# A two-layer diffusion step on one core: w_ffn_in token by token, with the activations stationary and the weights moving, and TensorE transposes behind it

## The chip, the cores and the metric

The kernel runs on 1 core of one Trainium2 chip. The metric is the device time of one execution in microseconds; less is better. The time of the kernel before is the median of 3 runs.

## The reference, cut to what matters

Two layers run over 128 context tokens and 128 latent tokens, 256 tokens in all, with D_MODEL = 2048 and D_FF = 5632. The change lies in the feed-forward part at the end of each layer:

```python
h = rms_norm(x, lp['ln_ffn']) * (1.0 + sc2) + sh2
gate, up = jnp.split(h @ lp['w_ffn_in'], 2, axis=-1)
x = x + g2 * ((jax.nn.silu(gate) * up) @ lp['w_ffn_out'])
```

All data are float32. `w_ffn_in` is 2048 x 11264 and `w_ffn_out` 5632 x 2048 in each layer.

## The kernel before

**Layout.** Activations lie transposed in SBUF: channels on the 128 partitions, the 256 tokens along the row (`xT`, 16 tiles of 128 channels). A matrix product gives out the transposed result, 128 output channels on the partitions and 256 tokens along the row, so that the next product can contract over channels again.

**Three products for one.** Every large product is split into a high and a low part. ScalarE rounds a weight tile `w` to `wh` (`act`, L155), VectorE takes `wl = w - wh` (`tt`, L128), in `weights`. The activations come as `hh` and `hl` (for `w_ffn_in`) or `ah` and `al` (for `w_ffn_out`). `block` in `gemm_steps` then issues three matmuls for one output: high by high, low activations by high weights, high activations by low weights. Each matmul instruction is two on TensorE, a load of the stationary operand (PEld) and the stream of the moving one (PE).

**`gemm_steps`.** It takes the rows of the weight matrix in tiles of 128 (16 steps for `w_ffn_in`), each up to 1024 columns wide. A step fetches and converts the tile of the next step, issues the matmuls of its own and may run a piece of another stream (`mod_tick`). Sums stay in up to four PSUM banks `pg` (pool `ps_g`, 4 buffers) through all steps. In the last step (`tail`) the banks are finished one after the other and each is handed to the evict function. A plan's entry (bank, offset, width, kind, column) says what a block does: kind `"w"` holds 128 weight columns stationary and moves 256 tokens; kind `"t0"` or `"t1"` holds 128 tokens stationary and moves `width` weight columns. `w_in` has used the second kind all along for the two banks of the GLA values (32 steps in the two layers), with 512 columns.

**The feed-forward part** (L1161 to L1217) goes through D_FF in three segments of 16, 16 and 12 tiles of 128 channels, and a segment in two groups of n = 8, 8 or 6 tiles. Each group is one product for the gate columns and one for the up columns, 128 n columns each. `ev_gate_ff` puts Silu of a gate bank into `sg` (ScalarE). `ev_up` multiplies `sg` by the up bank (VectorE), rounds it to `ah` (ScalarE) and takes `al` (VectorE). After both groups two products with `w_ffn_out` use `ah` and `al` as they are.

**Order of the work.** Each engine runs its own list in order; a framework sets the lists from the program's order and its own estimates. Weight tiles arrive through five buffers and are converted into five pairs `wh`, `wl`. Beside the products, VectorE works through the modulation matrices (`macc`, L288), four instructions for each slice of 128 rows, at a rate that `mod_tick` counts in weight tiles.

Of the kernel before, what the change touches and what calls it, by code (L numbers as in the profile page):

```python
# [17 lines left out]
KT = D // 128  # L18
# [85 lines left out]
def tile_backbone(ctx, tc, T, O):  # L104
# [22 lines left out]
    def tt(out, a, b, op):  # L127
        r = nc.vector.tensor_tensor(out=out, in0=a, in1=b, op=op)  # L128
        dve["last"] = r.ins.name
        return r  # L130
# [16 lines left out]
    def act(out, a, func=AF.Copy, **k):  # L147

        name = table_of.get(func)
        if name is not None and name != table["name"]:  # L150
            ld = nc.scalar.preload_act_table_set(name)
            for u in table["users"]:
                tc.add_manual_dep(ld.ins, u, no_sync, reason="table")
            table.update(name=name, load=ld.ins.name, users=[])
        r = nc.scalar.activation(out=out, in_=a, func=func, **k)  # L155
        if name is not None:
            tc.add_manual_dep(r.ins, table["load"], no_sync, reason="table")
            table["users"].append(r.ins.name)
        return r
# [8 lines left out]
    def px(shape):  # L168
        return ps_x.tile(shape, F32, tag="x", name="px")
# [85 lines left out]
    def early_run(l, m, kts, after):  # L255

        ps, w = early[l, m]
        for kt in kts:
            wv = quads(w[kt])
            for q in range(4):  # L260
                r = mm(ps[32 * q:32 * q + 32, :], sc[:, kt], wv[:, q], start=(kt == 0), stop=False)
                tc.add_manual_dep(r.ins, after, no_sync, reason="order")
# [84 lines left out]
    def gemm_steps(cols, tiles, x, plan, evict, pieces=None, pre=None, tail=1, quiet=0, done=None):  # L347

        ncol = sum(ap.shape[1] for ap in cols)
        nb = max(p[0] for p in plan) + 1  # L350
        banks = [ps_g.tile([128, 512], F32, tag="g", name="pg") for _ in range(nb)]
        byb = [[p for p in plan if p[0] == b] for b in range(nb)]
        nt = len(tiles)
        ahead = []

        def fetch(ti):
            if ti < nt:
                ahead.append(weights(cols, tiles[ti][0], ncol, pieces))

        def block(b, ti, wh, wl, a, c):  # L360
            ps = byb[b]
            for i, (_, off, width, kind, lc) in enumerate(ps):
                o = banks[b][:, off:off + width]
                if kind == "w":
                    sh, sl = wh[:, lc:lc + 128], wl[:, lc:lc + 128]
                    trip = ((sh, a), (sh, c), (sl, a))
                else:
                    t = slice(int(kind[1]) * 128, int(kind[1]) * 128 + 128)
                    mh, ml = wh[:, lc:lc + width], wl[:, lc:lc + width]
                    trip = ((a[:, t], mh), (c[:, t], mh), (a[:, t], ml))  # L370
                for j, (lt, rh) in enumerate(trip):
                    mm(o, lt, rh, start=(ti == 0 and i == 0 and j == 0),
                       stop=(ti == nt - 1 and i == len(ps) - 1 and j == 2))

        fetch(0)
        held = []
        for ti, (row, kt) in enumerate(tiles):
            fetch(ti + 1)
            wh, wl = ahead.pop(0)
            if pre is not None:  # L380
                pre(kt)
            a, c = x(kt)
            if ti >= nt - tail:
                held.append((ti, wh, wl, a, c))
            else:
                for b in range(nb):
                    block(b, ti, wh, wl, a, c)
            if ti < nt - quiet:
                mod_tick(ncol / 1024)
            yield  # L390
        for b in range(nb):
            for h in held:
                block(b, *h)
            if done is not None and b == nb - 1:
                done()
            evict(b, banks[b])
        dve["evict"] = dve["last"]

    def gemm(*args, **kw):
        for _ in gemm_steps(*args, **kw):  # L400
            pass
# [18 lines left out]
    def k_tiles(order):  # L420
        return [(128 * i, i) for i in order]

    def plan_w(n, lc0=0, b0=0):
        return [(b0 + i // 2, (i % 2) * 256, 256, "w", lc0 + 128 * i) for i in range(n)]
# [44 lines left out]
    def norm_mod(pool, l, msc, msh):  # L469
        new_h()  # L470
        hh, hl = normed["hh"], normed["hl"]

        def pre(k):
            t = pool.tile([128, 256], F32, tag="nt", name="nt", bufs=2)
            for g in range(2):
                s = slice(g * 128, g * 128 + 128)
                b = modv[:, l, msh, k, g:g + 1]
                stt(t[:, s], xT[:, k, s], modv[:, l, msc, k, g:g + 1], rstd[:, s], ALU.mult, ALU.mult)
                act(hh[:, k, s], t[:, s], AF.Identity, bias=b)
                stt(hl[:, k, s], t[:, s], b, hh[:, k, s].bitcast(F32), ALU.add, ALU.subtract)  # L480
        return pre
# [509 lines left out]
    for l in range(DEPTH):  # L991
# [168 lines left out]

        with PR(f"ff{l}") as fp:  # L1161
            f0 = 0
            for seg, nkt in enumerate((16, 16, 12)):
                parts = []
                done_kt = 0
                while done_kt < nkt:
                    n = 8 if nkt == 16 else 6
                    c0 = f0 + 128 * done_kt
                    sg = {}

                    def ev_gate_ff(b, bank):
                        sg[b] = fp.tile([128, 512], F32, tag="sg", name="sg", bufs=5)
                        act(sg[b], bank, AF.Silu)

                    def ev_up(b, bank):
                        ah = fp.tile([128, 2, 256], F32R, tag="ah", name="ah", bufs=8)
                        al = fp.tile([128, 2, 256], F32R, tag="al", name="al", bufs=8)
                        parts.append((ah, al))
                        s = sg[b]
                        tt(s, s, bank, ALU.mult)  # L1180
                        sv = s.rearrange("p (a t) -> p a t", a=2)
                        act(ah, sv)
                        tt(al, sv, ah.bitcast(F32), ALU.subtract)

                    pre = norm_mod(fp, l, 4, 3) if f0 == 0 and done_kt == 0 else None
                    w = T["w_ffn_in"][l]
                    gemm([w[:, c0:c0 + 128 * n]], k_tiles(range(KT)), hT, plan_w(n), ev_gate_ff, pre=pre, quiet=16 if pre else 0)
                    gemm([w[:, D_FF + c0:D_FF + c0 + 128 * n]], k_tiles(range(KT)), hT, plan_w(n), ev_up)
                    done_kt += n

                def aT(k):
                    h, lo = parts[k // 2]
                    return h[:, k % 2], lo[:, k % 2]

                if seg == 0:
                    mod_flush((l, 5))
                last_seg = seg == 2
                if last_seg:
                    ss = SquareSum(fp, l == DEPTH - 1)
                    if l == DEPTH - 1:  # L1200
                        yt = accp.tile([128, 2, D], F32, tag="macc", name="yt")
                for r in range(2):
                    def ev_ff(b, bank, r=r):
                        k = 8 * r + 2 * b
                        residual(l, 5, bank, k)
                        if last_seg:
                            ss.add(k, on_pe=(k >= KT - 6), last=(k == KT - 2))
                            if l == DEPTH - 1:
                                final_transpose(fp, k, yt)

                    tiles = [(f0 + 128 * i, i) for i in range(nkt)]
                    nxt = last_seg and r and l < DEPTH - 1
                    if nxt:
                        early_load(l + 1, 3)
                    gemm([T["w_ffn_out"][l][:, 1024 * r:1024 * r + 1024]], tiles, aT, plan_w(8), ev_ff, tail=2 if last_seg and r else 1,
                         quiet=QUIET if nxt else 0,
                         done=(lambda: early_run(l + 1, 3, range(1), pe["last"])) if nxt else None)  # L1217
                f0 += 128 * nkt
            mod_flush(*ffd)
            if l < DEPTH - 1:  # L1220
                early_run(l + 1, 3, range(1, EARLY), pe["last"])
                rsq(rstd, ss.ps, ss.acc[:, 0:256])
            else:
                final_scale(fp, ss, yt)
# [31 lines left out]
```

## Time and profile before

| | |
|---|---|
| median of 3 runs | 2512.47 us (2510.18 to 2515.29) |
| the profiled execution's own time | 2501.59 us |
| its span in the trace | 2499.6 us |
| TensorE matmul (PE) busy | 2442.9 us, 98% of the span |
| TensorE weight load (PEld) busy | 2245.2 us, 90% |
| VectorE (DVE) busy | 1656.6 us, 66% |
| ScalarE (ACT) busy | 1031.2 us, 41% |
| granted TensorE clock, mean | 0.997 |

The busy time of PE is the time in which at least one matmul was under way. Matmuls overlap: one lasts far longer than the distance to the next, so what a matmul costs in a stream is the distance between two starts. The profiled execution was 10.9 us shorter than the median of the runs.

### The profile page before, as it was taken

What the parts mean: (1) busy time and instruction counts of PE and PEld (TensorE: products, weight loads), DVE (VectorE), ACT (ScalarE), POOL (GpSimd) and SP (SyncE); (2) the same over time, 40 slices, a digit from 0 to 9 for tenths busy, and PEclk for the clock granted to TensorE, in tenths of its full rate; (3) what the DMA queues carried; (4) which work ended last, traced back from release to release, by engine and by line L of the source; (5) the groups of instructions that cost most, each with busy time, mean ns of one, the idle gap of its engine ahead of it and who ended that gap; (6) DMA issues with size and microseconds to landing.
All of it is one profiled execution on the core that took longest, in us unless ns stands there. A gap on an engine that the chain in (4) does not pass through costs nothing.

```text
span 2499.6 us, 47125 instructions
## 1 busy us (share of the span) xinstructions
PE 2442.9 (98%) x19685; PEld 2245.2 (90%) x19685; DVE 1656.6 (66%) x2367; ACT 1031.2 (41%) x1405; POOL 0.2 (0%) x4
## 2 busy tenths in 40 slices
PE   6999999999999999999999999999999999999998
PEld 3666767999999999999998887899999999999998
DVE  3665555887879888888858555598655545454455
ACT  2334433454443334334446444345444334433443
POOL 0000000000000000000000000000000000000000
PEclk9999999999999999999999999999999999999999
DMA  8988788867778778677956667686755566555662
GB/s 302 334 311 307 279 296 319 330 222 250 244 244 295 263 250 303 226 266 264 318 197 195 220 221 257 236 308 202 236 178 184 179 186 186 178 187 167 183 202 96
DMA packets 167304, 601.20 MB, mean 241 GB/s; under 512 B 18576, under 2 KB 24882, under 8 KB 146612
## 3 DMA queue, kind: packets, MB, share of 16 engines
q1 hardware_dynamic: 164104, 592.27, 70.3%
q10 hardware_dynamic: 2988, 5.93, 0.7%
q8 instruction: 154, 2.52, 0.4%
q14 instruction: 58, 0.48, 0.1%
HBM read 592.03 MB, written 6.09 MB: 239 GB/s over the span
## 4 chain that ended last, share of the span: by engine, by line
PE 93%; DMA 4%; DVE 2%; ACT 1%; issue 0%; SPq 0%; ACTq 0%; DVEq 0%
PE pg L164 81%; PE px L164 8%; PE mps L164 4%; DMA mw<-in_w_mod_dram 3%; DMA xin<-in_x_prompt_dram 0%; DVE wl L128 0%; PE px L948 0%; ACT e L155 0%; DVE xT L133 0%; DMA rows<-in_ln_ffn_dram 0%; ACT wh L155 0%; DMA w<-in_w_in_dram 0%; PE px L977 0%; DVE st L934 0%; DMA rows<-in_hy_filt_b_dram 0%
## 5 line engine op out<-in xcount | busy, mean ns | idle before, releaser
L128 DVE TENSOR_TENSOR wl<-w,wh 128x1024 fp32r<-128x1024 f32 (+3 forms) x816 | 872.1, 1085 | 579.4 <-ACT wh L155 573.6
L155 ACT ACTIVATE wh<-w 128x1024 fp32r<-128x1024 f32 (+3 forms) x816 | 767.0, 949 | 1130.7 <-PE pg L164 975.3
L164 PE MATMUL pg<-hh,wh 128*128 128x256 f32 x3648 | 1039.0, 286 | 3.7 <-ACT hh L155 2.6
L164 PE MATMUL pg<-hl,wh 128*128 128x256 f32 x3648 | 1034.7, 284 | 0.0
L164 PE MATMUL pg<-hh,wl 128*128 128x256 f32 x3648 | 1032.2, 284 | 2.5 <-DVE wl L128 2.5
L164 PEld LDWEIGHTS pg<-hh,wh 128*128 128x128 f32 x3648 | 696.6, 191 | 41.6 <-issue 26.1
L164 PEld LDWEIGHTS pg<-hl,wh 128*128 128x128 f32 x3648 | 697.9, 191 | 10.4 <-issue 8.8
L164 PEld LDWEIGHTS pg<-hh,wl 128*128 128x128 f32 x3648 | 696.5, 191 | 11.5 <-issue 6.8
L164 PE MATMUL pg<-ah,wl 128*128 128x256 f32 x1408 | 395.3, 281 | 0.0
L164 PE MATMUL pg<-al,wh 128*128 128x256 f32 x1408 | 395.3, 281 | 0.0
L164 PE MATMUL pg<-ah,wh 128*128 128x256 f32 x1408 | 395.1, 282 | 0.0
L288 DVE SCALAR_TENSOR_TENSOR macc<-mw,sc,macc 128x1024 f32<-128x1024 f32 x268 | 331.6, 1278 | 0.5 <-DMA mw<-in_w_mod_dram 0.5
L164 PEld LDWEIGHTS pg<-ah,wh 128*128 128x128 f32 x1408 | 264.7, 188 | 1.7 <-ACT wh L155 1.7
L164 PEld LDWEIGHTS pg<-al,wh 128*128 128x128 f32 x1408 | 265.6, 189 | 0.1
L164 PEld LDWEIGHTS pg<-ah,wl 128*128 128x128 f32 x1408 | 264.8, 188 | 0.1
L164 PE MATMUL mps<-mw,sc 128*32 128x512 f32 (+1 forms) x1216 | 143.1, 537 | 17.7 <-DMA mw<-in_w_mod_dram 17.7
L164 PEld LDWEIGHTS mps<-mw,sc 128*32 128x32 f32 x1216 | 29.7, 112 | 73.6 <-issue 36.8
L133 DVE SCALAR_TENSOR_TENSOR xT<-pg,modv,xT 128x128 f32<-128x128 f32 x256 | 69.6, 342 | 27.4 <-PE pg L164 27.3
L164 PE MATMUL pg<-ymh,wh 128*128 128x256 f32 x256 | 72.3, 286 | 1.9 <-DVE xT L133 1.9
L164 PE MATMUL pg<-ymh,wl 128*128 128x256 f32 x256 | 71.5, 283 | 0.6 <-DVE wl L128 0.6
L164 PE MATMUL pg<-yml,wh 128*128 128x256 f32 x256 | 72.1, 283 | 0.0
L164 PEld LDWEIGHTS pg<-ymh,wh 128*128 128x128 f32 x256 | 48.8, 192 | 5.1 <-issue 2.9
(285 smaller groups left out, 1838.1 us busy)
## 6 DMA issues: line engine op xcount, KB each, us to landing
mw<-in_w_mod_dram SPq DMA_DIRECT2D x160, 1024.0 KB
w<-in_w_ffn_in_dram SPq DMA_DIRECT2D x256, 512.0 KB
w<-in_w_ffn_out_dram SPq DMA_DIRECT2D x176, 512.0 KB
w<-in_w_ffn_in_dram SPq DMA_DIRECT2D x128, 384.0 KB
mw<-in_w_mod_dram SPq DMA_DIRECT2D x64, 512.0 KB
w<-in_w_in_dram SPq DMA_DIRECT2D x64, 512.0 KB
w<-in_w_out_dram SPq DMA_DIRECT2D x64, 512.0 KB
w<-in_w_in_dram SPq DMA_DIRECT2D x64, 256.0 KB
```

The lines of the kernel that those rows point to most:

```text
L128: r = nc.vector.tensor_tensor(out=out, in0=a, in1=b, op=op)
L133: r = nc.vector.scalar_tensor_tensor(out=out, in0=a, scalar=s, in1=b, op0=op0, op1=op1)
L155: r = nc.scalar.activation(out=out, in_=a, func=func, **k)
L164: r = nc.tensor.matmul(*args, **kw)
L288: r = nc.vector.scalar_tensor_tensor(out=acc[:, i, cs], in0=w[:, cs], scalar=c, in1=acc[:, i, cs], op0=ALU.mult, op1=ALU.add)
```

## The change

`w_ffn_in` uses the second kind of block: the 128 tokens of each half (t0: context, t1: latent) are held stationary, and up to 512 weight columns move. A bank now holds 128 tokens on the partitions and 512 (n = 8) or 384 (n = 6) channels along the row; there are four banks for either n (before: three for n = 6). `w_ffn_out` needs channels on the partitions again, so `turn` transposes each finished 128 x 128 piece on TensorE into a PSUM tile `px` and makes `ah` and `al` from there. The four turns of a group are kept in a list `late`; `run_late` runs one after each step of the following products, from the second step on.

```diff
             f0 = 0
+            late = []
+
+            def run_late(steps):
+
+                for i, _ in enumerate(steps):
+                    if late and i:
+                        late.pop(0)()
+
...
+                    wd = 64 * n
+
                     def ev_gate_ff(b, bank):
                         sg[b] = fp.tile([128, 512], F32, tag="sg", name="sg", bufs=5)
-                        act(sg[b], bank, AF.Silu)
+                        act(sg[b][:, :wd], bank[:, :wd], AF.Silu)
 
                     def ev_up(b, bank):
-                        ah = fp.tile([128, 2, 256], F32R, tag="ah", name="ah", bufs=8)
-                        al = fp.tile([128, 2, 256], F32R, tag="al", name="al", bufs=8)
-                        parts.append((ah, al))
                         s = sg[b]
-                        tt(s, s, bank, ALU.mult)
-                        sv = s.rearrange("p (a t) -> p a t", a=2)
-                        act(ah, sv)
-                        tt(al, sv, ah.bitcast(F32), ALU.subtract)
-
+                        tt(s[:, :wd], s[:, :wd], bank[:, :wd], ALU.mult)
+                        late.append(lambda: turn(b, s))
+
+                    def turn(b, s, n=n, wd=wd, halves=[None, None]):
+
+                        t, half = divmod(b, 2)
+                        if t == 0:
+                            ah = fp.tile([128, 4, 256], F32R, tag="ah", name="ah", bufs=4)
+                            al = fp.tile([128, 4, 256], F32R, tag="al", name="al", bufs=4)
+                            halves[half] = ah, al
+                            parts.extend((ah[:, j], al[:, j]) for j in range(n // 2))
+                        ah, al = (v[:, :n // 2, 128 * t:128 * t + 128] for v in halves[half])
+                        p = px([128, 4, 128])[:, :n // 2]
+                        for j in range(n // 2):
+                            nc.tensor.transpose(p[:, j], s[:, 128 * j:128 * j + 128], ident)
+                        act(ah, p)
+                        tt(al, p, ah.bitcast(F32), ALU.subtract)
+
+                    plan = [(2 * t + i, 0, wd, f"t{t}", wd * i) for t in range(2) for i in range(2)]
...
-                    gemm([w[:, c0:c0 + 128 * n]], k_tiles(range(KT)), hT, plan_w(n), ev_gate_ff, pre=pre, quiet=16 if pre else 0)
-                    gemm([w[:, D_FF + c0:D_FF + c0 + 128 * n]], k_tiles(range(KT)), hT, plan_w(n), ev_up)
+                    run_late(gemm_steps([w[:, c0:c0 + 128 * n]], k_tiles(range(KT)), hT, plan, ev_gate_ff, pre=pre, quiet=16 if pre else 0))
+                    run_late(gemm_steps([w[:, D_FF + c0:D_FF + c0 + 128 * n]], k_tiles(range(KT)), hT, plan, ev_up))
...
                 def aT(k):
-                    h, lo = parts[k // 2]
-                    return h[:, k % 2], lo[:, k % 2]
+                    return parts[k]
```

The products with `w_ffn_out` keep their plan and are driven by `run_late` too.

On TensorE's list, in a step of `w_ffn_in` with n = 8, these rows stand before the change (moving operand first behind the arrow, then the stationary one; the numbers tell buffers apart). A bank takes six of them and a step has four banks:

```order
L164 MATMUL pg_5398<-hh_5394,wh_5926 128x256
L164 MATMUL pg_5398<-hl_5395,wh_5926 128x256
L164 MATMUL pg_5398<-hh_5394,wl_5927 128x256
L164 MATMUL pg_5399<-hh_5394,wh_5926 128x256
L164 MATMUL pg_5399<-hl_5395,wh_5926 128x256
L164 MATMUL pg_5399<-hh_5394,wl_5927 128x256
```

With the change, the end of the second step of the second group's gate product, the first turn of the first group's `sg` and the start of the third step read:

```order
L164 MATMUL pg_6132<-wh_6141,hh_5394 128x512
L164 MATMUL pg_6132<-wh_6141,hl_5395 128x512
L164 MATMUL pg_6132<-wl_6142,hh_5394 128x512
L1202 MATMUL px_6177<-ident_81,sg_5791 128x128 x4
L164 MATMUL pg_6129<-wh_6159,hh_5394 128x512
L164 MATMUL pg_6129<-wh_6159,hl_5395 128x512
L164 MATMUL pg_6129<-wl_6160,hh_5394 128x512
```

Three rows of 512 columns stand where six of 256 stood, weights and activations have changed sides, and four transposes stand between two steps.

On VectorE's list these rows stood at the end of the first group's up product in layer 0:

```order
L128 TENSOR_TENSOR sg<-sg,pg 128x512
L128 TENSOR_TENSOR wl<-w,wh 128x1024
L128 TENSOR_TENSOR al<-sg,ah 128x512
L128 TENSOR_TENSOR sg<-sg,pg 128x512 x3
L128 TENSOR_TENSOR al<-sg,ah 128x512 x3
L128 TENSOR_TENSOR wl<-w,wh 128x1024
L288 SCALAR_TENSOR_TENSOR macc<-mw,sc,macc 128x1024 x4
L128 TENSOR_TENSOR wl<-w,wh 128x1024 x8
```

With the change the same place reads:

```order
L128 TENSOR_TENSOR sg<-sg,pg 128x512
L128 TENSOR_TENSOR wl<-w,wh 128x1024
L128 TENSOR_TENSOR sg<-sg,pg 128x512 x3
L128 TENSOR_TENSOR wl<-w,wh 128x1024
L288 SCALAR_TENSOR_TENSOR macc<-mw,sc,macc 128x1024 x4
L128 TENSOR_TENSOR al<-px,ah 128x4x128
L128 TENSOR_TENSOR wl<-w,wh 128x1024 x2
L128 TENSOR_TENSOR al<-px,ah 128x4x128
```

The four multiplications stay where they were, and the four subtractions for `al` have moved behind the block of `macc` and between the conversions of later weight tiles.

## Rows read from the trace of the kernel before

**Rows 1.** The page, busy time (us), share of the span and instructions of an engine.
```profile
PE 2442.9 (98%) x19685; PEld 2245.2 (90%) x19685; DVE 1656.6 (66%) x2367; ACT 1031.2 (41%) x1405; POOL 0.2 (0%) x4
```
**Rows 2.** The chain that ended last, in order of time: start us, us, what.
```profile
542.95 115.61 PE pg L164 x960
...
660.42 194.00 PE pg L164 x1632
...
1837.01 609.17 PE pg L164 x5082
```
**Rows 3.** Timeline of PE, w_ffn_in, layer 0: start us, us, engine, line, instruction.
```profile
1236.01 0.28 PE L164 MATMUL pg<-hh,wh 128*128 128x256 f32 x1
...
1236.97 0.28 PE L164 MATMUL pg<-hh,wl 128*128 128x256 f32 x1
```
**Rows 4.** Timeline of PE, w_in, layer 1: GLA values between weight-stationary blocks.
```profile
1364.61 0.40 PE L164 MATMUL pg<-wh,hh 128*128 128x512 f32 x1
...
1366.00 0.28 PE L164 MATMUL pg<-hh,wh 128*128 128x256 f32 x1
...
1402.24 0.40 PE L164 MATMUL pg<-wh,hh 128*128 128x512 f32 x1
1402.48 0.39 PE L164 MATMUL pg<-wh,hl 128*128 128x512 f32 x1
...
1403.61 0.28 PE L164 MATMUL pg<-hh,wh 128*128 128x256 f32 x1
```
**Rows 5.** Timeline of PE, attention of layer 1: a run of 384-column matmuls.
```profile
1395.15 0.34 PE L164 MATMUL px<-kyl,uk 128*128 128x384 f32 x1
...
1397.07 0.40 PE L164 MATMUL px<-uk,kyh 128*128 128x256 f32 x2
```
**Rows 6.** Timeline of PE, attention of layer 1: transposes between matmuls.
```profile
1406.43 0.82 PE L948 MATMUL px<-ident,e 128*128 128x128 f32 x6
1407.01 0.36 PE L164 MATMUL pg<-hh,wh 128*128 128x256 f32 x1
1407.21 0.28 PE L164 MATMUL pg<-hl,wh 128*128 128x256 f32 x1
...
1381.84 0.76 PE L948 MATMUL px<-ident,e 128*128 128x128 f32 x5
1382.35 0.47 PE L164 MATMUL pg<-wh,hh 128*128 128x512 f32 x1
1382.66 0.39 PE L164 MATMUL pg<-wh,hl 128*128 128x512 f32 x1
```
**Rows 7.** Instructions of line 977: duration of one in ns, min/median/max, first and last start.
```profile
L977 PE MATMUL px<-ident,xl x32: 270/273/328, 2446.0 to 2489.9; 128*128 128x128 f32 x32
```
**Rows 8.** Timeline of DVE at the end of the first up product, layer 0.
```profile
633.40 0.69 DVE L128 TENSOR_TENSOR sg<-sg,pg 128x512 f32<-128x512 f32 x1 [1.40 <-PE pg L164]
...
635.74 1.88 DVE L128 TENSOR_TENSOR sg<-sg,pg 128x512 f32<-128x512 f32 x3
...
640.47 4.87 DVE L288 SCALAR_TENSOR_TENSOR macc<-mw,sc,macc 128x1024 f32<-128x1024 f32 x4
645.26 4.62 DVE L128 TENSOR_TENSOR wl<-w,wh 128x1024 fp32r<-128x1024 f32 x4
```
**Rows 9.** Windows: from:to, us, busy and count of PE, PEld, DVE, ACT, POOL; PEclk, DMA share, GB/s.
```profile
870.00:990.00 120.00, 120.00 (x1003) 120.00 (x1002) 104.59 (x94) 49.07 (x50) 0.00 (x0) 1.00 0.81 284
1110.00:1230.00 120.00, 120.00 (x1001) 119.94 (x1000) 107.25 (x108) 53.64 (x66) 0.00 (x0) 1.00 0.83 293
...
760.00:810.00 50.00, 50.00 (x429) 50.00 (x428) 46.74 (x53) 19.12 (x18) 0.00 (x0) 1.00 0.82 291
```
**Rows 10.** Groups by line and shape, 487 to 1313 us: busy, mean ns | idle before, releaser.
```profile
L155 ACT ACTIVATE sg<-pg 128x512 f32<-128x512 f32 x22 | 13.0, 590 | 0.8
L128 DVE TENSOR_TENSOR sg<-sg,pg 128x512 f32<-128x512 f32 x22 | 14.2, 683 | 7.5 <-PE pg L164 7.5
```

More of the change, by code (lines that the diff above doesn't have):

```diff
@@ L1214, in tile_backbone @@
                         early_load(l + 1, 3)
-                    gemm([T["w_ffn_out"][l][:, 1024 * r:1024 * r + 1024]], tiles, aT, plan_w(8), ev_ff, tail=2 if last_seg and r else 1,
+                    run_late(gemm_steps([T["w_ffn_out"][l][:, 1024 * r:1024 * r + 1024]], tiles, aT, plan_w(8), ev_ff, tail=2 if last_seg and r else 1,
                          quiet=QUIET if nxt else 0,
-                         done=(lambda: early_run(l + 1, 3, range(1), pe["last"])) if nxt else None)
+                         done=(lambda: early_run(l + 1, 3, range(1), pe["last"])) if nxt else None))
                 f0 += 128 * nkt
```

## The prediction

> **What bounds the kernel now.** I read the busy times first: TensorE has a matmul under way for 2442.9 of 2499.6 us, VectorE is busy for 66% and ScalarE for 41% [rows 1]. So only what TensorE does can shorten the run, as long as the others keep up. The chain of waits in order of time says the same of the feed-forward part: the pieces there are TensorE alone, 194.0 us and 609.2 us without a break, across w_ffn_in and w_ffn_out alike [rows 2]. Nothing is waited for there, so the change is worth what it takes from or adds to TensorE's own stream.
>
> In that stream a matmul lasts 280 ns, but the next one starts long before it ends; the cost is the distance between starts. In w_ffn_in eight distances make 0.96 us, 120.0 ns for 256 columns [rows 3]. A window inside one such product counts 1003 in 120 us, of which two or three only reach in over the edges [rows 9]. The piece of 960 that holds the start of the layer gives 115.61 / 960 = 120.4 ns [rows 2]. I use 120.0.
>
> **What goes and what comes on TensorE.** w_ffn_in has 88 column tiles of 128, 16 row tiles, 3 products, 2 layers: 8448 matmuls of 256 columns, 1013.8 us. Of these 6144 belong to groups with n = 8 and 2304 to n = 6. The change makes 3072 matmuls of 512 columns from the first and 1536 of 384 columns from the second. The columns moved are as many as before, the instructions fewer by 3840.
>
> *512 columns.* The trace has this very form, in w_in: weights moving, hh and hl stationary, six in a row between blocks of the old form. One run takes 1366.00 - 1364.61 = 1.39 us for six, 231.7 ns each; another 1403.61 - 1402.24 = 1.37 us, 228.3 ns, and the last five of it, behind the step over from the old form, 1403.61 - 1402.48 = 1.13 us, 226 ns [rows 4]. In the changed kernel the form goes on for 44 us at a time, and runs of six always hold the step over. So I take the faster run, 228.3 ns, and keep 226 and 231.7 as bounds. Saved: 6144 x 0.1200 - 3072 x 0.2283 = 737.3 - 701.3 = **36.0 us** (25.5 to 43.0).
>
> *384 columns.* A run of them in the attention goes from 1395.15 to 1397.07 in 11 distances (the rows between count ten more), 174.5 ns [rows 5]. Saved: 2304 x 0.1200 - 1536 x 0.1745 = 276.5 - 268.0 = **8.4 us**. Its bounds are small beside the others.
>
> *Transposes.* 44 channel tiles, two token halves, two layers: 176 of 128 x 128, in 32 turns of four and 16 of three. I price them with the step over to them and back. Six of them start at 1406.43 and the second matmul behind them at 1407.21; that is 0.78 us less the one distance of 0.12 that would be there anyway, 0.66 us or 110 ns each. Five ahead of a 512-column matmul: 1382.66 - 1381.84 = 0.82 less 0.23, 0.59 us or 118 ns each [rows 6]. I take 115 ns: 176 x 0.115 = **20.2 us** added (19.4 to 20.8).
>
> Here a rule of the Trainium skill speaks against the change. The rows give 110 to 118 ns for a transpose in a stream [rows 6], although one lasts 273 ns from start to end [rows 7]. The Trainium skill (TensorE: Matmul & The Clock Gate, Part 4: PE-mode transpose) gives about 275 ns for a transpose in a kernel's context. By 275 ns they would cost 48.4 us, an estimate from that page, and the change would lose some 4 us. The trace agrees with 275 as the time from start to end and not as the distance.
>
> **What moves on the other engines, priced at nothing.** The rounding to ah, the subtraction for al, Silu and the multiplication are as many elements as before; ah and al now read PSUM.
>
> - *VectorE keeps up.* In w_ffn_in of layer 0 it is busy for 104.59 of 120 us with n = 8 and 107.25 of 120 with n = 6 [rows 9]. The same work in a time shorter by 4.9% and 3.1% makes 92% of both. In w_ffn_out it is at 46.74 of 50 us, 93%, and TensorE is at work for all 50 of them [rows 9]. So the trace already shows a stage as tight as the new one without a wait. The DMA share, 0.81 and 0.83, rises to 0.86 at most.
> - *The turn finds its data.* At the end of an up product VectorE starts its first multiplication as bank 0 ends, and the last three are done by 635.74 + 1.88 = 637.62, 4.2 us later [rows 8]; with al moved behind, about 3.6 us. TensorE meanwhile finishes three banks (9 x 0.228 = 2.1 us) and two steps of the next product (2 x 2.74 us) before its first transpose, 7.5 us behind bank 0. The cover is 3.9 us. Behind the turn, the next matmul needs wl; VectorE's block of four macc (4.87 us, then conversions from 645.26, 11.9 us behind bank 0 [rows 8]) stands where it stood, and fewer instructions are ahead of it now.
> - *Four banks for n = 6.* There is no spare bank any more. A bank must be read before the next product starts on it, 9 x 0.1745 = 1.57 us later. ScalarE needs 0.59 us and VectorE 0.68 us for it [rows 10]. If a macc instruction (4.87 / 4 = 1.22 us) has just begun, it is 1.9 us, 0.3 us late: 4 up products, 1.3 us at most. I take 0.
>
> **Sum.** 36.0 + 8.4 - 20.2 = 24.2 us less, with bounds 25.5 + 8.4 - 20.8 - 1.3 = 11.8 and 43.0 + 8.4 - 19.4 = 32.0. The profiled execution of 2501.6 us becomes 2477.4 us. That execution was 10.9 us shorter than the median of the runs, 2512.5 us, so the forecast for a median is **2488 us**, with 2480 to 2501 by the bounds. A measurement of this kernel can tell some 0.2%, 5 us, from no change.
>
> **Rivals.**
>
> 1. *Each transpose costs its whole length.* If the matmul behind a transpose had to wait for its end, 176 x 0.273 = 48.0 us [rows 7] would meet a gain of 44.4 us: 3.6 us slower, 2516 us, within 0.2%. (It is what the rule of the Trainium skill, TensorE: Matmul & The Clock Gate, Part 4, comes to.) Against it stand both runs of rows 6; for it, that none of them has four transposes ahead of a long stream. 5%.
> 2. *The pace is set by columns, not by instructions.* Should the long stream of 512 take twice 120 ns, and 384 columns 180, nothing is saved, and the transposes remain: 20.2 us slower, 2533 us. It decides from 512 columns at 240 - (20.2 - 8.4) / 3.072 = 236.2 ns on, with 384 as priced. For it: the old form itself does not keep one pace; in w_ffn_out the same 256 columns go at 50 / 427, 117 ns [rows 9], so something beside the form matters, and stationary activations may bring their own. Against it: the runs of six lie at 228 to 232 with hh and hl stationary [rows 4]. 9%.
> 3. *VectorE comes late to the turns.* If it reaches the multiplications later by more than the cover of 3.9 us, TensorE stands at the first turn of each of the 12 groups. One block of macc too late (4.87 us [rows 8]) costs 1.0 us a group, 12 us: 2500 us, still faster. To undo the gain it takes 2 us in each group. Against it: VectorE itself waited 7.5 us for TensorE ahead of its multiplications in layer 0 [rows 10], so it comes early. 8% that it takes enough to land within 0.2%, or a little behind.
>
> **How the numbers follow.** The forecast's own case has 78%: it holds 2480 to 2501. Rival 1 has 5%, rival 2 9%, rival 3 8%. The range for 8 in 10 is 2476 to 2505: the bounds, and 4 us on either side for the scatter of medians (the runs before span 5.1 us). Faster by over 0.2% (under 2507): the 78% and a part of rival 3, 81%. Within 0.2%: rival 1 and most of rival 3, 9%. Slower: rival 2 and the end of rival 3, 10%.
>
> **What the changed profile would show.** Right: in w_ffn_in starts of 512-column matmuls 226 to 232 ns apart and of 384 ones near 174, granted clock 1.0; a turn of four transposes puts 0.45 us between two steps; the chain in the feed-forward part is still TensorE alone, the part of layer 0 shorter by some 12 us, that of layer 1 by as much. Wrong: a pace over 236 ns; idle time of PE ahead of px with VectorE's sg as releaser, or ahead of pg with wl; starts behind a transpose 0.27 us apart; a granted clock under 1.0 in these stretches.

## The result and the profile after

The changed kernel takes 2475.87 us (median of 4 runs, 2474.91 to 2477.44). The kernel before took 2513.88 us beside it (4 runs, 2510.18 to 2518.00). The ratio is 0.9848, with a 95% interval of 0.9834 to 0.9863: **faster, by 38 us in this comparison**. The forecast was 2488 us with a range from 2476 to 2505; the time lies 12.1 us below the forecast and 0.13 us below the lower end of the range. The profiled execution took 2476.38 us.

The page of the kernel after gives the busy times that answer to [rows 1]:

```profile
PE 2416.0 (98%) x16021; PEld 2094.0 (85%) x16021; DVE 1657.0 (67%) x2375; ACT 1026.8 (41%) x1413; POOL 0.2 (0%) x4
```

3664 instructions are gone from TensorE: 3840 matmuls fewer, 176 transposes more. It is still at work for 98% of the span, so the time came out of its own stream, and none of it went into idle time. TensorE's waits from 487 to 1300 us, the feed-forward part of layer 0 and a little ahead of it (waiting engine and line, for whom: us in total, times, longest), are these three and no more:

```profile
PE pg L164 <- DVE xT L133: 1.9, 2, 1.7
PE pg L164 <- DVE wl L128: 0.6, 1, 0.6
PE pg L164 <- DVE nt L133: 0.6, 1, 0.6
```

None is for `sg` ahead of a turn, and the single wait for `wl` is 0.6 us. In layer 1, from 1600 us to the end, there are three waits more, the longest of 1.0 us, and none of them is for `sg`, `wl` or a turn. The chain that ended last (start us, us, what) answers to [rows 2]:

```profile
549.18 92.88 PE pg L164 x408
642.07 0.44 PE px L1202 x4
642.50 2.76 PE pg L164 x12
645.26 0.44 PE px L1202 x4
...
733.34 0.44 PE px L1202 x4
733.78 2.85 PE pg L164 x24
```

It is TensorE alone, as before, now cut by the turns (a *turn* is the group of three or four transposes that `turn` issues). The first 408 matmuls of 512 columns take 92.88 / 408 = 227.6 ns each, the start included. A turn of four takes 0.44 us; the turns of a segment's last group stand in `w_ffn_out`, where a step has 24 matmuls of 256 columns.

The timeline of PE (start us, us, engine, line, instruction) shows a turn, then a stretch of 512 columns and one of 384 far from any turn:

```profile
641.67 0.40 PE L164 MATMUL pg<-wl,hh 128*128 128x512 f32 x1
641.90 0.60 PE L1202 MATMUL px<-ident,sg 128*128 128x128 f32 x4
642.26 0.48 PE L164 MATMUL pg<-wh,hh 128*128 128x512 f32 x1
642.57 0.39 PE L164 MATMUL pg<-wh,hl 128*128 128x512 f32 x1
...
899.81 0.39 PE L164 MATMUL pg<-wh,hh 128*128 128x512 f32 x1
...
904.57 0.39 PE L164 MATMUL pg<-wh,hh 128*128 128x512 f32 x1
...
1139.73 0.33 PE L164 MATMUL pg<-wl,hh 128*128 128x384 f32 x1
...
1143.89 0.33 PE L164 MATMUL pg<-wl,hh 128*128 128x384 f32 x1
```

Between 899.81 and 904.57 lie 21 distances: **226.7 ns** each, where the forecast took 228.3 (in longer stretches, of 300 to 480 matmuls and behind the first five of each, it is 226.7 to 227.0, and I use 226.9). Between 1139.73 and 1143.89 lie 24: **173.3 ns**, against 174.5. The windows answer to [rows 9] (columns as there):

```profile
870.00:990.00 120.00, 120.00 (x539) 99.16 (x538) 105.92 (x94) 50.16 (x52) 0.00 (x0) 1.00 0.83 292
1110.00:1230.00 120.00, 120.00 (x708) 119.86 (x707) 107.77 (x111) 55.45 (x71) 0.00 (x0) 1.00 0.84 294
```

The granted clock is 1.00 in both, as before. VectorE is at 88% and 90%, the DMA share at 0.83 and 0.84, TensorE without a gap.

A stretch goes from the start of a product's first matmul to the start of the next product's (the last one to the end of the span). Summed over its six stretches, `w_ffn_in` went from 1020.5 to 980.2 us and `w_ffn_out` from 532.9 to 543.3 us: 30 us in all, 14.3 in layer 0 and 15.7 in layer 1, where the forecast had some 12 in each. `w_ffn_out` became longer because half of the turns stand in it, 9.7 us by their rows.

### The profile page after: what moved, and what is told of

Same layout as the page of the kernel before. It is cut to its first block, busy times and chain, and to the rows that moved or that the text cites. A ratio compares the mean times of both kernels' runs of the same rounds, so it can differ in the third digit from the quotient of the medians.

```text
span 2474.4 us, 39841 instructions
## 1 busy us (share of the span) xinstructions
PE 2416.0 (98%) x16021; PEld 2094.0 (85%) x16021; DVE 1657.0 (67%) x2375; ACT 1026.8 (41%) x1413; POOL 0.2 (0%) x4
## 4 chain that ended last, share of the span: by engine, by line
PE 93%; DMA 4%; DVE 2%; ACT 1%; issue 0%; SPq 0%; DVEq 0%; ACTq 0%
PE pg L164 79%; PE px L164 8%; PE mps L164 4%; DMA mw<-in_w_mod_dram 3%; PE px L1202 1%; DVE wl L128 0%; PE px L948 0%; ACT e L155 0%; DMA w<-in_w_in_dram 0%; DVE xT L133 0%; DMA fdec<-in_decay_dram 0%; DVE nt L133 0%; ACT wh L155 0%; PE px L977 0%; DVE st L934 0%
## 5 line engine op out<-in xcount | busy, mean ns | idle before, releaser
L128 DVE TENSOR_TENSOR wl<-w,wh 128x1024 fp32r<-128x1024 f32 (+3 forms) x816 | 873.4, 1086 | 549.1 <-ACT wh L155 543.3
L164 PE MATMUL pg<-wh,hh 128*128 128x512 f32 (+1 forms) x1600 | 597.2, 374 | 1.1 <-DVE nt L133 1.1
L164 PE MATMUL pg<-wh,hl 128*128 128x512 f32 (+1 forms) x1600 | 595.6, 372 | 0.0
L164 PE MATMUL pg<-wl,hh 128*128 128x512 f32 (+1 forms) x1600 | 594.5, 372 | 0.0
L164 PEld LDWEIGHTS pg<-wh,hl 128*128 128x128 f32 x1600 | 300.5, 188 | 41.0 <-issue 0.3
L164 PE MATMUL pg<-hh,wh 128*128 128x256 f32 x832 | 244.3, 295 | 2.6 <-ACT hh L155 1.3
L164 PE MATMUL pg<-hh,wl 128*128 128x256 f32 x832 | 236.8, 288 | 3.7 <-DVE wl L128 3.7
L164 PE MATMUL pg<-hl,wh 128*128 128x256 f32 x832 | 239.0, 288 | 0.0
L164 PEld LDWEIGHTS pg<-hh,wh 128*128 128x128 f32 x832 | 159.2, 192 | 35.4 <-issue 26.7
L164 PEld LDWEIGHTS pg<-hh,wl 128*128 128x128 f32 x832 | 158.5, 192 | 13.3 <-issue 6.8
L164 PEld LDWEIGHTS pg<-hl,wh 128*128 128x128 f32 x832 | 159.7, 192 | 10.8 <-issue 9.4
```

The costliest lines, as they stand in the source:

```text
L164: r = nc.tensor.matmul(*args, **kw)
```

## The experiments

**The theory**: the gain is TensorE's stream alone, fewer matmuls at a fixed cost beside their columns, less some 110 ns for each transpose; what goes beyond it comes from the draw of the runs, that is from which executions a median happens to hold. **The rivals**: a transpose costs more than its place in the stream; it is the form (activations stationary), not the number of matmuls, that pays; the kernel before was slower in some stage at the timed runs than in its profile; the changed kernel has a longer head of its own. *Head* is the time from the start to the first product of `w_ffn_in` in layer 0, in which the change alters no instruction of TensorE; the rest is the span less the head.

### Both kernels again, unchanged

Seven runs, without an edit. The first two:

> The kernel before, unchanged, profiled and timed once more. In the two profiles the changed stages gave back 30 us, the spans 25 us and the timed medians 38 us; this run asks where the other differences lie. Theory H (the head varies): the part ahead of the first product of w_ffn_in, 543.0 us in the profile of before and 549.2 in that of after though nothing in it is changed, differs from execution to execution, and the first profile of before caught a short one. Then this profile's span is longer than 2499.6 by just what its head is longer, with 1956.6 us from the head's end to the end, and the timed runs spread over 8 us or more. Rival P (timed runs of the kernel before are longer than profiled ones): the profile is near 2500 again with a head near 543, and the timed median near 2513. Rival S (the stages themselves vary): the part behind the head is longer than 1956.6 by more than 3 us.

> The changed kernel, unchanged, once more. Theory H: behind the head 1925.2 us as in its first profile, a head that may differ from 549.2 by some us, the span by the same. Rival P: span 2474 and median 2476 with the same head. Rival S: the part behind the head differs by more than 3 us.

After a third time, beside more runs of before:

> The changed kernel, unchanged, a third time, beside more runs of the kernel before. In its two profiles the head waited 20.0 and 18.4 us for the modulation weights, in the two of before 14.0 and 14.0. Theory H (chance): a head like before's turns up, near 543 us, and the difference of the medians is 28 to 33 us. Rival P (the changed program has a head that is longer by 4 us whenever it runs): head near 549 again.

And each kernel twice more, in turn on one chip:

> The kernel before once more, unchanged, for its head: the time from the start to the first product of w_ffn_in, in which both kernels issue the same instructions. So far it ended at 543.0 and 545.9 us in two profiles of before and at 549.2, 550.2 and 548.0 in three of after. Theory C (chance): the head varies from execution to execution whatever the kernel, and four looks in turn on one chip overlap: this one ends its head anywhere from 543 to 551 us. Rival K (the kernel): the changed kernel has a longer head of its own; then this one ends at 543 to 546 and both looks at after at 548 to 551. In both, what lies behind the head takes 1957 us, within 1.5.

> The changed kernel once more, unchanged. Theory C: the head ends anywhere from 543 to 551 us. Rival K: 548 to 551. In both, what lies behind it takes 1925 to 1928 us.

> The kernel before a second time on the same chip. Theory C: head anywhere from 543 to 551 us, and the two heads of before differ from one another by as much as from those of after. Rival K: 543 to 546, 3 us or more ahead of both looks at after. Behind the head 1957 us, within 1.5.

> The changed kernel a second time on the same chip. Theory C: head anywhere from 543 to 551 us. Rival K: 548 to 551. Behind the head 1925 to 1928 us. If K holds, the change gives 28 us and not 31; if C holds, 31 us is what it gives, and the rest of the measured difference is the draw of the runs.

Measured by time: 2508.69 us for before again (11 runs, ratio to before 1.0004, 0.9995 to 1.0013), 2480.07 us for after again (4 runs beside 18 of before at 2508.66; ratio 0.9883, 0.9870 to 0.9896) and 2475.85 us for after once more (5 runs beside 11 of before at 2509.12; ratio 0.9877, 0.9861 to 0.9893). So three comparisons give 38.0, 28.6 and 33.3 us. By profile, us:

| profiled execution | time | span | head | rest |
|---|---|---|---|---|
| before | 2501.59 | 2499.6 | 542.95 | 1956.6 |
| r1_before_again | 2505.65 | 2503.6 | 545.89 | 1957.7 |
| s1_before | 2516.46 | 2514.4 | 552.51 | 1961.9 |
| s3_before | 2510.04 | 2508.0 | 548.45 | 1959.6 |
| after | 2476.38 | 2474.4 | 549.18 | 1925.2 |
| r2_after_again | 2480.03 | 2478.1 | 550.21 | 1927.9 |
| r3_after_once_more | 2474.93 | 2473.0 | 547.98 | 1925.0 |
| s2_after | 2483.12 | 2481.2 | 553.60 | 1927.6 |
| s4_after | 2476.22 | 2474.4 | 545.93 | 1928.5 |

The end of the head is the start of one row of the chain; for the longest head of before and the shortest of after:

```profile
552.51 115.61 PE pg L164 x960
```

```profile
545.93 92.88 PE pg L164 x408
```

The heads of the two kernels overlap (543.0 to 552.5, and 545.9 to 553.6), so a head that is always longer with the change is out; a difference of 1 or 2 us in the mean isn't excluded by nine heads. Expectations were missed on the way: r3_after_once_more was to show a head near 543 us if chance alone were at work, and showed 548.0, so that only the four runs in turn decided; and two heads of these lie beyond the 551 us expected. The head is the largest part of what varies from one execution of a kernel to the next. The rest was expected within 1.5 us; it spreads by 5.3 and 3.5 us, wider than I had thought: in s1_before and s4_after the part of layer 1 between its first product and its product with `w_out` took 302.5 us, elsewhere 298.6 to 301.6. No stage of `w_ffn_in` in before is slower in one profile than in another by over 0.2 us, so for the changed product the rival of a slower stage is out. For the stages around it, it is not: `w_ffn_out` took from 532.9 to 536.3 us in the four profiles of before, and the rest of s1_before, 5.3 us longer than the first, is beyond the 3 us from which r1_before_again counted this rival as true.

The medians of the rest, 1958.7 and 1927.6 us, differ by **31 us, which I take for what the change gives**; by the spread of these nine values that holds to some 3 us (an estimate). All executions of the two kernels taken together agree: the 48 of before have a mean of 2509.5 us and the 15 of after one of 2478.1, 31.4 us less. The profile shown ahead of the prediction was the fastest of the 48 executions of before, 2501.59 us beside medians of 2508.7 to 2513.9. The 95% intervals of the first and the second comparison (0.9834 to 0.9863, and 0.9870 to 0.9896) don't overlap: the interval of one comparison doesn't hold the scatter between comparisons. Whether chance or the chip makes this scatter wasn't tested.

What makes the head vary is only partly seen. TensorE's wait for modulation weights in it, by the list of waits, is 14.0 us in the profile of before and 20.0 in that of after, which is 6.0 of the 6.2 us between these two heads; but s2_after has the longest head with 14.9 us of it. The windows over the shortest and the longest head, before and s2_after (columns as in [rows 9]), show another part:

```profile
0.00:542.95 542.95, 504.01 (x3797) 375.43 (x3797) 331.35 (x639) 201.89 (x351) 0.20 (x4) 0.99 0.86 306
```

```profile
0.00:553.60 553.60, 509.61 (x3798) 381.67 (x3798) 331.01 (x638) 201.54 (x350) 0.20 (x4) 0.98 0.85 300
```

For the same instructions TensorE was at work 5.6 us longer, at a lower mean granted clock, 0.98 against 0.99. What lowered the clock in one execution and not in the other stays open.

### The transposes taken out

```diff
-                        p = px([128, 4, 128])[:, :n // 2]
-                        for j in range(n // 2):
-                            nc.tensor.transpose(p[:, j], s[:, 128 * j:128 * j + 128], ident)
+                        p = s[:, :wd].rearrange("p (j t) -> p j t", t=128)
```

`ah` and `al` are made from `sg` as it stands, so `w_ffn_out` gets tokens and channels the wrong way round; all other work stays.

> The changed kernel without its 176 transposes: ah and al are made straight from sg, so the product with w_ffn_out gets tokens and channels mixed up. By the starts in the changed profile the turns take 0.44 us each of four and 0.33 each of three, 19.5 us in all; the forecast had 20.2. Theory: 19 to 21 us faster than the changed kernel, 2456. Rival (a turn costs its whole lengths, 48 us): 2428. Rival (the transposes hide behind other work): within 5 us of 2476.

Measured: 2454.94 us (4 runs; ratio to before 0.9787, 0.9774 to 0.9799), 25.1 us below after on the same chip. In the profile the rest is 2456.2 - 550.2 = 1906.0 us, 19.0 to 22.5 below the five of after; the feed-forward parts alone take 1504.3 us, against a median of 1523.4: **19.1 us**. The chain runs through where the turns were:

```profile
550.20 109.20 PE pg L164 x480
```

480 matmuls, 227.5 ns each. At their whole length the transposes would have been worth 48.0 us; that rival is out. The medians gave 6 us more than the profile and than the 19 to 21 us expected; this run doesn't show why, and medians of one and the same kernel differ by as much, see above.

The run also shows the two savings without the transposes: its six stretches of `w_ffn_in` take 969.6 us, 50.9 less than before, 40.5 of them with n = 8 and 10.4 with n = 6.

### The transposes put into the kernel before

```diff
...
+                        late.append(lambda: turn(s))
+
+                    def turn(s):
+                        p = px([128, 4, 128])
+                        for j in range(4):
+                            nc.tensor.transpose(p[:, j], s[:, 128 * j:128 * j + 128], ident)
...
```

The products are driven by `run_late` as in after; nothing reads what the transposes write, and all of the computation stays as in before.

> The kernel before with 176 transposes of sg added between the steps, at the places where the changed kernel has its turns (44 groups of four); their result is read by nobody, the rest is as before. Theory: 0.44 us for each group of four, 19.4 us slower than before, near 2528 where before is 2508.7. Rival (part of the 0.44 us is the change of form around a turn, weights against activations stationary): a price other than 0.44 us a group by more than 0.05 us, 2 us in all.

Measured: 2532.00 us (6 runs; ratio 1.0091, 1.0074 to 1.0108), 22.9 us more. The feed-forward parts take 1574.0 us, against 1553.4 to 1556.8 in the four profiles of before: 17.2 to 20.6 us. The chain shows each turn of four at the price that it has in after:

```profile
645.24 0.44 PE px L1197 x4
645.68 2.88 PE pg L164 x24
648.56 0.44 PE px L1197 x4
```

44 x 0.44 = 19.4 us, as expected. So a transpose costs 110 ns in both streams, among 256 columns as among 512.

### The new form with half the columns

```diff
-                    plan = [(2 * t + i, 0, wd, f"t{t}", wd * i) for t in range(2) for i in range(2)]
+                    mv = wd // 2 if n == 8 else wd
+                    plan = [(2 * t + i, o, mv, f"t{t}", wd * i + o) for t in range(2) for i in range(2) for o in range(0, wd, mv)]
```

Activations stay stationary, but for n = 8 each matmul moves 256 weight columns, twice as many of them.

> The changed kernel with each product of 512 columns (n = 8) split into two of 256, stationary activations as before it. Theory N (a fixed 13 ns for each matmul beside its columns, so the number of matmuls is what pays): 120 ns for 256 columns, 256 steps x (24 x 0.120 - 12 x 0.2269) = 40.2 us slower than the changed kernel, 2516. Rival F (stationary activations are the quicker form at any width): about 113.5 ns for 256 columns, no change, 2476.

Measured: 2515.84 us (7 runs; ratio 1.0029, 1.0017 to 1.0041), 35.8 us more than after on the same chip; all of the gain is gone. The rest is 2512.9 - 547.1 = 1965.8 us, 38.2 above the median of after, and `w_ffn_in` takes 1019.6 us, against 1020.5 before. Its timeline of PE:

```profile
899.82 0.28 PE L164 MATMUL pg<-wl,hh 128*128 128x256 f32 x1
...
902.94 0.28 PE L164 MATMUL pg<-wh,hl 128*128 128x256 f32 x1
```

26 distances, **120.0 ns** each: what [rows 3] show for the form of before. At 256 columns it makes no difference which operand stands still; it is the number of matmuls that pays.

### Moves of 192 columns

The same edit with `n == 6` in place of `n == 8`: 192 columns, so that the distances of 192, 256, 384 and 512 columns could be set against each other.

> The changed kernel with each product of 384 columns (n = 6) split into two of 192. It asks what the fixed part of a matmul is. Theory N (columns at 2.4 GHz plus a fixed 13.3 ns for each matmul): 80 + 13.3 = 93.3 ns, 128 steps x (24 x 0.0933 - 12 x 0.1733) = 20.4 us slower than the changed kernel, 2500. Rival L (a weight load takes its own 120 ns, and no matmul stream goes below that, so that 256 columns sat on the load and not on a fixed part): 120 ns, 128 x (24 x 0.120 - 12 x 0.1733) = 102 us slower, 2582.

Measured: 2566.76 us (4 runs; ratio 1.0228, 1.0215 to 1.0241), 90.9 us more than after, between the two theories of it. The timeline of PE in layer 1, then around a turn in layer 0:

```profile
2302.05 0.27 PE L164 MATMUL pg<-wh,hh 128*128 128x192 f32 x1
...
2302.94 0.27 PE L164 MATMUL pg<-wl,hh 128*128 128x192 f32 x1
...
1189.21 0.27 PE L164 MATMUL pg<-wh,hl 128*128 128x192 f32 x1
...
1190.33 0.27 PE L164 MATMUL pg<-wl,hh 128*128 128x192 f32 x1
```

8 distances of 111 ns and 10 of 112. From 256, 384 and 512 columns (120.0, 173.3, 226.9 ns) a column costs 0.418 ns and a matmul 13 ns beside them; 192 would be 93 by that line. So the line breaks: there is a floor near 111 ns, and neither theory had it. The trace of before could have told. It has matmuls of 128 columns against a stationary operand of 128 x 128, two to a row:

```profile
1606.32 0.38 PE L164 MATMUL px<-mats,yim 128*128 128x128 f32 x2
...
1607.65 0.39 PE L164 MATMUL px<-mats,yim 128*128 128x128 f32 x2
```

12 distances, 111 ns each: 128 columns go no faster than 192, and a transpose, which moves 128 columns too, takes the same 110 ns.

The pace of 192 columns explains 3072 x 0.1112 - 1536 x 0.1733 = 75.4 us of the 90.9.

Most of what is left lies in one stage: with n = 6 `w_ffn_in` takes 187.5 us in layer 0 and 173.6 in layer 1. TensorE's waits there in layer 0, and VectorE's timeline at the longest of them:

```profile
PE pg L164 <- DVE wl L128: 4.4, 4, 1.6
PE px L1202 <- DVE al L128: 4.1, 1, 4.1
```

```profile
1190.38 7.26 DVE L288 SCALAR_TENSOR_TENSOR macc<-mw,sc,macc 128x1024 f32<-128x1024 f32 x6
1197.55 0.95 DVE L128 TENSOR_TENSOR wl<-w,wh 128x768 fp32r<-128x768 f32 x1
1198.42 0.55 DVE L128 TENSOR_TENSOR al<-px,ah 128x384 fp32r<-128x384 f32 x1
```

The `al` of the first turn stands behind two blocks of `macc` on VectorE's list, of two and of the six shown, and starts at 1198.42, though ScalarE began its `ah` at 1186.64. Until then its `px` isn't free, and the fourth turn waits for it. The windows around this stop show what the clock did:

```profile
1170.00:1190.00 20.00, 20.00 (x182) 20.00 (x181) 14.15 (x16) 7.23 (x10) 0.00 (x0) 1.00 0.50 142
1190.00:1210.00 20.00, 15.91 (x120) 15.74 (x118) 14.88 (x17) 4.36 (x7) 0.00 (x0) 0.83 0.72 253
1210.00:1230.00 20.00, 20.00 (x182) 20.00 (x181) 13.77 (x13) 6.97 (x9) 0.00 (x0) 1.00 0.57 159
```

The granted clock is 0.83 in the slice in which TensorE stood for 4.1 us, and 1.00 on both sides: 120 matmuls where its neighbours have 182, so 62 x 0.110 = 6.8 us were lost, 2.7 more than the stop. The timeline of PE behind the stop shows them:

```profile
1199.89 0.41 PE L164 MATMUL pg<-wh,hl 128*128 128x192 f32 x1
...
1204.37 0.41 PE L164 MATMUL pg<-wh,hl 128*128 128x192 f32 x1
```

These are 21 distances of 213 ns, nearly twice the 111, and the granted clock from 1200 to 1204 us is 0.50, the lower of its two levels. In after itself no turn waits.

### A version with groups of 8 and 4 tiles in the last segment

```diff
-                    n = 8 if nkt == 16 else 6
+                    n = min(8, nkt - done_kt)
+                    ng = 2 if n == 8 else 1
...
-                    wd = 64 * n
+                    wd = 128 * n // ng
...
-                    plan = [(2 * t + i, 0, wd, f"t{t}", wd * i) for t in range(2) for i in range(2)]
+                    plan = [(ng * t + i, 0, wd, f"t{t}", wd * i) for t in range(2) for i in range(ng)]
```

`turn` uses `ng` in place of 2. All matmuls of `w_ffn_in` then move 512 columns, 384 instructions fewer.

> The changed kernel with the last segment's 12 channel tiles as groups of 8 and 4 instead of 6 and 6, so that all products move 512 columns: 18 matmuls of 226.9 ns stand for 24 of 173.3 ns at each row tile of the segment. Theory N (a fixed 13.3 ns for each matmul): 4.084 against 4.159 us, 64 such pairs of steps, 4.8 us faster than the changed kernel, 2475. Rival (full banks and fewer, larger groups make VectorE or ScalarE late at the ends): same or slower than the changed kernel.

Measured: 2474.07 us (4 runs, 2465.88 to 2475.49; ratio to before 0.9852, 0.9836 to 0.9869, where after once more has 0.9877, 0.9861 to 0.9893). It beats the kernel before; that it beats after isn't shown, since 1.8 us is within what medians differ by. Its two stages went from 134.5 and 134.6 to 132.8 and 132.5 us, 3.8 of the 4.8 us expected.

## Why the prediction was wrong in size and right in kind

**What bounds the kernel: right.** It was TensorE's stream alone, and no other bound came in its place.

**The term for 512 columns: the step that failed.** The prediction argued that "runs of six always hold the step over" and took 228.3 ns from such a run, 36.0 us saved. In the changed kernel the stream goes on for 408 matmuls, with no step over between forms; it runs at 226.9 ns, nearly the pace of the last five of that run, 226 [rows 4], which I had kept as a bound only. 737.3 - 3072 x 0.2269 = **40.2 us**, and 40.5 by the stages of the run without transposes. The row for the long stream was at hand, and I had taken the mean over an end effect that the new stream doesn't have.

**384 columns: right in kind, 1.9 us small.** 173.3 ns, 276.5 - 1536 x 0.1733 = 10.3 us (10.4 by those stages), not 8.4. Eleven distances in the rows of before were too short a run for an error of 1 ns, and the prediction gave this term no bounds.

**Transposes: right.** 20.2 us were priced, 19.1 us came when they were taken out and 17.2 to 20.6 when they were put into before, so rival 1 is out. The Trainium skill's figure for a transpose (TensorE: Matmul & The Clock Gate, Part 4: PE-mode transpose), about 275 ns, is what one lasts in the trace from start to end, 272 ns in the median of the 176; the distance that it takes up in the stream is 110 ns.

The sum of the three with measured sizes is 40.2 + 10.3 - 19.1 = 31.4 us, not 24.2, and the profiles give 31 behind the head. That is within the bounds of the sum, 11.8 to 32.0, close to the upper one; the prediction stood nearer the middle.

**The base: the second part of the miss.** The prediction added 10.9 us to the forecast for the profiled execution, 2477.4 us, as the distance of that execution to a median of three. It was the distance between the fastest of 48 executions and a median on the high side (larger samples: 2508.7 and 2509.1 us), and after's profile has no such distance to its own median. In the comparison that was forecast the medians came 38.0 us apart, 7.0 more than the rest shows. So the miss of 12.4 us (from 2488.3 unrounded) is 6.8 of terms (31.0 less 24.2) and 7.0 beyond them, less 1.4 by which before came out longer than in the runs shown. That the 7.0 us are a draw is argued from the spread of the executions; the timed runs of before in that comparison have no trace, and the cause of the 7.0 stays open. The 4 us allowed for the scatter of medians were too few: three comparisons of the same two kernels span 9.4 us.

**What was priced at nothing: right.** VectorE's last multiplications ahead of the first turn in after are these:

```profile
636.24 1.88 DVE L128 TENSOR_TENSOR sg<-sg,pg 128x512 f32<-128x512 f32 x3
```

They end at 638.12 us, the turn starts at 641.90: a cover of 3.8 us, where 3.9 was worked out. TensorE doesn't wait for VectorE at any turn, so rival 3 is out for this kernel, and it doesn't wait for a bank with n = 6. But this is a matter of VectorE's order: in the run with 192 columns six `macc` came ahead of an `al`, and a turn stood for 4.1 us until its `px` was free, a wait that the prediction didn't list.

**Rival 2, the pace set by columns**, is out: 226.9 ns, against the 236.2 from which it would decide.

## What to carry to other kernels

Where TensorE is the bound and never waits, count instructions as well as columns: here each matmul cost 13 ns beside its columns from 256 upwards, so 3840 fewer gave some 50 us, and a transpose took 110 ns of the stream, though it lasted 272. Price a form that will run in long streams by the inner distances of its longest run in the trace, without the step into it. By the profiles, behind the head, the change gave 31 us, while medians of a few runs put the same change at 28.6 to 38.0: a range for such a median needs that scatter on top of the bounds of the terms.

## What was not expected of the hardware

- The distance of matmuls has a floor: 128 columns took 111 ns and 192 columns 111 to 112, hardly less than 256 at 120.0. What sets it wasn't measured by itself.
- Behind a turn the first matmul takes 0.31 us (642.26 to 642.57), against 0.227 in the stream, and the next ones 0.23.
- `w_ffn_out`, with activations moving, goes at 118.6 ns for 256 columns in after (35 distances from 2209.74 to 2213.89 us in its timeline), a little under the 120.0 of `w_ffn_in` before, and the prediction had read 117 for it in before. What sets it stays open.
- The head, the same work in both kernels, took 543 to 554 us over nine profiles.
